# Weight sums of the block-product passes made in the pooling stage, and the passes' first operands split inside the mLSTM

## The chip, the cores and the metric

The kernel runs on one core of a Trainium2 chip. The metric is the device time of one execution in microseconds (us); the figure for a kernel is the median of its runs. A profiled execution of its own gives the trace from which all durations are read. The core's engines are TensorE (PE, matmuls and transposes, its weight loads shown as PEld), VectorE (DVE), ScalarE (ACT), GpSimd (POOL) and SyncE (SP). SP and ACT issue the DMAs, each in a queue of its own that runs in order.

## The reference

One layer of a decoder trunk over 4096 tokens of width 1024, in float32: a normalization, one input projection to 5120 columns, two branches that read it, one output projection, the residual, and a last normalization.

```python
u = rmsnorm(x, norm_w[l])
proj = u @ w_in[l]                      # 1024 -> 5 * 1024
pool_x, pool_z, m_x, m_z, m_o = ...     # 1024 columns each
y_pool = pool_mixer(pool_x, pool_w[l], pool_scale[l]) * jax.nn.silu(pool_z)
y_mlstm = mlstm_branch(m_x, m_z, m_o, ...)
mixed = jnp.concatenate([y_pool, y_mlstm], axis=-1)
x = x + mixed @ w_out[l]                # 2048 -> 1024
return rmsnorm(x, final_norm_w)

# in mlstm_branch, behind the chunkwise recurrence that gives h:
h = jax.nn.sigmoid(mo) * h
hn = ((h - mu) * lax.rsqrt(var + EPS)) * mh_norm_w     # mu, var per head
out = (hn + m_skip * xc) * jax.nn.silu(mz)
```

## The kernel before

**Precision.** A float32 product is made of three matmuls. `split` writes a tile as a rounded part `hi` (a cast on ACT, L110) and the remainder `lo` (a subtraction on DVE, L111); `mm3` (L117 to L119) adds hi·hi, hi·lo and lo·hi in PSUM.

**Stage A, pooling.** Eight blocks `b` of 512 tokens, each with eight column steps `j`. A block normalizes its tokens (`norm_u`), stores them as quarters into `us_d`, and makes the projections, the trailing window sums (DVE), the gate (ACT) and the product `sg`, which is stored into `yp_d`. Beside it `sums` (loads L493, subtractions L500 to L506 on POOL, stores L497) makes the sums of quarters that the block products need on the left side, for pairs of blocks that are done. The last of these jobs, `sums(yp_d[-1], 2)`, stands behind the loop.

**Stage B, mLSTM.** 32 chunks of 128 tokens. The weights `wm` of m_x are loaded through tiles `ws` (load L127, 16 loads of 256 KB, two buffers) and split. `project` loads `u` (L700), splits it (ACT L702, POOL L703) and multiplies; `front` and `back` are the two halves of a chunk, and the tuple `ORDER` says in which order the steps of front, back and projection are written down. L740 and L750 are the first map matmuls of `front`, L867 and L871 matmuls of `back`, L885 the activation that closes a head. In the last chunks, the generator `next_weights` takes the projection's place: it loads the first four right operands of C's first pass, as sums of up to four quarters, added on POOL (L129).

**Stage C, four passes.** `drive` runs the passes o1 (left side `yp_d`, with the first half of w_out), mo and mz (left side `us_d`, columns of w_in) and o2 (left side `ym_d`, second half of w_out). Each is a product of 2 x 2 blocks with seven block products (Strassen–Winograd, so that sums of quarters are needed on both sides), over four row bands `r`, seven products `i` and two halves `kh`: 14 half-steps a band, 24 matmuls of 512 columns each. For half-step `t` the left operand `sr` of half-step `t + 3` is loaded (`issue`, a DMA on ACT's queue, L223), and that of `t + 2` is split (`make`). `defer` puts work off to the end of the half-step. The right operands of the next pass are loaded in the last band of the pass before. `Pass.stage` (loads L155, POOL L159 to L162, stores L165) computes the sums of quarters of the right sides of mo and mz in bands 0 to 2 of o1, and those of o2 in mz, and stores them in `sums_...`; o1's own sums are made as they are loaded (L127, L129).

In pass mo an item `Head` finishes a block: tanh, product with `h`, the mean and variance (DVE L1035 to L1040 with a power on POOL L1038), and the normalization (ACT L1043). Each head block is then turned with transposes on TensorE (L1069), multiplied and added on DVE (L1071) with `xc` (L1062) and stored. The table `FREE_BANKS` says after which half-step of a band how many such turned tiles (four transposes each) are put into the program.

Two properties of the build matter for the order of the DMAs. A scheduler places instructions within each engine, so the order in a queue can differ from the order in the code. And the DMAs of SP and ACT share a small set of completion semaphores: the issue of a DMA waits for the landing of the one that used its semaphore last.

Of the kernel before, what the change touches and what calls it, by code (L numbers as in the profile page):

```python
# [17 lines left out]
P = 128  # L18
# [25 lines left out]
B_OF = (((1, 0, 0),),  # L44
        ((1, 1, 1), (-1, 0, 1), (1, 0, 0)),
        ((1, 1, 0),),
        ((1, 1, 1), (-1, 0, 1)),
        ((1, 0, 1), (-1, 0, 0)),
        ((1, 1, 0), (-1, 1, 1), (1, 0, 1), (-1, 0, 0)),
        ((1, 1, 1),))  # L50
SUM_OF = (None, 1, None, 2, 0, 3, None)

FREE_BANKS = {6: 2, 7: 2, 11: 3, 12: 3, 13: 3, 0: 3, 1: 2}
# [7 lines left out]
def tile_hybrid(  # L61
# [59 lines left out]
    def load_right(hi, lo, k, terms, sources, tile):  # L121

        acc = None
        for sign, kh, ch in terms:
            t = tile()
            rows, c0 = sources[ch]
            nc.sync.dma_start(out=t, in_=rows(k + 4 * kh)[:, c0:c0 + T])  # L127
            if acc is not None:
                nc.gpsimd.tensor_tensor(out=acc, in0=acc, in1=t, op=ALU.add if sign > 0 else ALU.subtract)  # L129
            else:  # L130
                acc = t
        split(acc, hi[:, k], lo[:, k])

    class Pass:


        def __init__(self, name, left, sources, items, by_row):

            self.name, self.left, self.sources, self.items, self.by_row = name, left, sources, items, by_row
            self.slots = {}  # L140
            self.sums = None
# [4 lines left out]
        def stage(self, k, tile):  # L146

            if self.sums is None:
                self.sums = dram.tile([4, P, 4, T], F32, name=f"sums_{self.name}")
            q = {}  # L150
            for kh in range(2):
                for ch in range(2):
                    rows, c0 = self.sources[ch]
                    q[kh, ch] = tile()
                    nc.sync.dma_start(out=q[kh, ch], in_=rows(k + 4 * kh)[:, c0:c0 + T])  # L155
            t3 = tile()
            yield
            b11, b12, b21, b22 = q[0, 0], q[0, 1], q[1, 0], q[1, 1]
            nc.gpsimd.tensor_tensor(out=t3, in0=b22, in1=b12, op=ALU.subtract)  # L159
            nc.gpsimd.tensor_tensor(out=b12, in0=b12, in1=b11, op=ALU.subtract)  # L160
            nc.gpsimd.tensor_tensor(out=b22, in0=b22, in1=b12, op=ALU.subtract)
            nc.gpsimd.tensor_tensor(out=b21, in0=b21, in1=b22, op=ALU.subtract)  # L162
            yield
            for i, t in enumerate((b12, b22, t3, b21)):
                nc.sync.dma_start(out=self.sums[i][:, k, :], in_=t)  # L165

        def load(self, i, pool, tag, tile):

            self.slots[i] = hi, lo = [pool.tile([P, 4, T], F32R, name=tag) for _ in range(2)]
            for k in range(4):  # L170
                if SUM_OF[i] is None or self.sums is None:
                    load_right(hi, lo, k, B_OF[i], self.sources, tile)
                elif k % 2 == 0:
                    raw = lo[:, k:k + 2].bitcast(F32)
                    nc.sync.dma_start(out=raw, in_=self.sums[SUM_OF[i]][:, k:k + 2, :])
                    split(raw, hi[:, k:k + 2], lo[:, k:k + 2])
                yield
# [34 lines left out]
    def drive(passes, ring, slot_pool, tile, psp, background):  # L212
# [13 lines left out]
        def make(t):  # L226
            if t < len(steps):
                hi, lo = got[t]
                split(lo.bitcast(F32), hi, lo)

        def load(p, i):
            for _ in p.load(i, *slot_pool(i), tile):
                pass
# [5 lines left out]
        def prefetch():  # L239
            while later and len(fetched) < 3:  # L240
# [4 lines left out]
        for t in range(AHEAD - 1):  # L245
            issue(t)
        for t in range(AHEAD - 2):
            make(t)
        for t, (n, r, i, kh) in enumerate(steps):
            p = passes[n]  # L250
            issue(t + AHEAD - 1)
            if n + r == 0:
                miss = [v for v in range(NP) if v not in p.slots]
                if miss and miss[0] <= t // 2 + 4:
# [11 lines left out]
            for q in range(4):  # L266
                ps = banks[chain, q]
                pairs = []
                for k in range(2):
                    kk = 2 * kh + k  # L270
                    if p.by_row:
                        pairs.append((tuple(z[:, k, q * P:(q + 1) * P] for z in s), tuple(z[:, kk, :] for z in w)))
                    else:
                        pairs.append((tuple(z[:, kk, q * P:(q + 1) * P] for z in w), tuple(z[:, k, :] for z in s)))
# [76 lines left out]
    ab = ExitStack()  # L351
    stp = ab.enter_context(tc.tile_pool(name="stp", bufs=4))
    wsp = ab.enter_context(tc.tile_pool(name="wsp", bufs=2))
# [29 lines left out]
    with tc.tile_pool(name="a_u", bufs=19) as up, \  # L383
# [124 lines left out]

        wz, wg = [], []
# [8 lines left out]
        job = None  # L518
        jobs = []
        for b in range(NB):  # L520
# [6 lines left out]
            for j in range(NJ):  # L527
# [8 lines left out]
                nc.gpsimd.tensor_copy(out=halo[:, j, :], in_=z[:, T:])  # L536
                pz = accp.tile([P, T], F32, name="acc")
# [36 lines left out]
        for _ in sums(yp_d[-1], 2):  # L574
# [3 lines left out]
    p_out1 = Pass("o1", yp_d, halves(out_rows(0), 0), [], True)  # L578
    with tc.tile_pool(name="b_one", bufs=1) as one, \
# [635 lines left out]
```

## Time and profile before

| | us |
|---|---|
| median of 3 runs (lowest, highest) | 3157.94 (3155.6, 3158.84) |
| profiled execution | 3153.02 |
| its span | 3151.3 |
| TensorE busy | 2919.7 |
| A's last matmul starts | 752.29 |
| first front of B | 820.85 |
| B's last matmuls start | 1757.23 |
| first matmul of C | 1770.93 |
| first matmul of mo, of mz, of o2 | 2115.1, 2495.7, 2815.9 |

The busy time of an engine is an average over stages that have different limits: in A TensorE is busy without a break, in B the small operations of the recurrence share the time, and in C TensorE is busy but for single stretches. In a row of the timeline the first two numbers are the start and the length, and the bracket at the end holds the idle time before and what ended it. In the rows of groups the last column is that idle time summed up.

### The profile page before, as it was taken

Reading aid. Unit: us, or ns where it says so; the run is one execution under the profiler, and the core shown is the slowest. Engines: PE = TensorE matmul, PEld = TensorE weight load, DVE = VectorE, ACT = ScalarE, POOL = GpSimd, SP = SyncE. Lnnn points to the kernel's source line nnn. Section 1 sums busy time; section 2 is a strip of 40 time slices with the busy share of each in tenths; the row PEclk is TensorE's granted clock in tenths of the full one; section 3 lists DMA queues with packets and bytes.
Section 4 is the critical chain, followed back from the end, with each engine's and each line's share of the span. In section 5 each row is a group of like instructions: output and inputs, shape, how many; then the busy total and the mean of one; then the engine's idle time right before and its main releaser. Section 6 shows DMA issues by size and latency. Waiting matters only on the chain. (4 is left out here: it accounts for less than half of the span.)

```text
span 3151.3 us, 45085 instructions
## 1 busy us (share of the span) xinstructions
PE 2919.7 (93%) x15912; PEld 2522.1 (80%) x15912; DVE 2089.8 (66%) x4160; ACT 1373.6 (44%) x2727; POOL 960.7 (30%) x1015
## 2 busy tenths in 40 slices
PE   7999999996989999999997788999998899998998
PEld 6888888885989989989897566887777688876887
DVE  6555555544578878888888553566667766575666
ACT  4222122211577677767666311235556633342332
POOL 1122333333245455445445432001111145321000
PEclk9999999998899999999998899999999999998999
DMA  6344455556121121111113688765666788786654
GB/s 211 124 153 159 155 181 184 184 174 201 46 64 51 48 68 48 61 55 51 61 58 111 227 309 268 238 225 192 209 218 230 260 273 302 260 290 208 213 208 157
DMA packets 256419, 530.55 MB, mean 168 GB/s; under 512 B 28352, under 2 KB 71872, under 8 KB 256192
## 3 DMA queue, kind: packets, MB, share of 16 engines
q1 hardware_dynamic: 223936, 410.21, 37.6%
q10 hardware_dynamic: 32256, 117.45, 11.9%
q8 instruction: 125, 2.05, 0.3%
q14 instruction: 102, 0.84, 0.1%
HBM read 334.63 MB, written 192.94 MB: 167 GB/s over the span
## 5 line engine op out<-in xcount | busy, mean ns | idle before, releaser
L117 PE MATMUL acc<-u,w 128*128 128x512 f32 (+1 forms) x2016 | 691.6, 343 | 2.2 <-ACT u L110 1.8
L119 PE MATMUL acc<-u,w 128*128 128x512 f32 (+1 forms) x2016 | 682.4, 339 | 0.0
L118 PE MATMUL acc<-u,w 128*128 128x512 f32 (+1 forms) x2016 | 680.7, 338 | 0.0
L117 PE MATMUL ps<-w,sr 128*128 128x512 f32 x1344 | 536.7, 399 | 44.4 <-ACT sr L110 29.6
L119 PE MATMUL ps<-w,sr 128*128 128x512 f32 x1344 | 533.6, 397 | 9.2 <-DVE sr L111 9.0
L118 PE MATMUL ps<-w,sr 128*128 128x512 f32 x1344 | 532.5, 396 | 0.0
L111 DVE TENSOR_TENSOR sr<-sr 128x1024 fp32r<-128x1024 f32 x224 | 293.5, 1314 | 304.3 <-ACT sr L110 299.4
L110 ACT CAST sr<-sr 128x1024 fp32r<-128x1024 f32 x224 | 234.2, 1048 | 552.0 <-PE ps L118 293.6
L117 PEld LDWEIGHTS acc<-u,w 128*128 128x128 f32 x2016 | 383.7, 190 | 44.3 <-ACT u L110 2.5
L118 PEld LDWEIGHTS acc<-u,w 128*128 128x128 f32 x2016 | 383.7, 190 | 40.3
L119 PEld LDWEIGHTS acc<-u,w 128*128 128x128 f32 x2016 | 383.5, 190 | 40.2
L117 PEld LDWEIGHTS ps<-w,sr 128*128 128x128 f32 x1344 | 257.9, 192 | 99.6 <-ACT sr L110 32.3
L119 PEld LDWEIGHTS ps<-w,sr 128*128 128x128 f32 x1344 | 257.1, 191 | 69.5 <-DVE sr L111 16.7
L118 PEld LDWEIGHTS ps<-w,sr 128*128 128x128 f32 x1344 | 257.6, 192 | 53.5 <-issue 0.5
L656 DVE SCALAR_TENSOR_TENSOR xc<-mx,col,xc 128x256 f32<-128x256 f32 x384 | 221.2, 632 | 55.4 <-POOL mx L715 46.4
L644 POOL TENSOR_TENSOR cs<-c,cs 128x516 fp32r<-128x516 f32 x124 | 176.4, 1422 | 204.2 <-ACT cs L643 181.7
L1038 POOL TENSOR_TENSOR rs<-rs,nhalf 128x2 f32<-128x2 f32 x64 | 56.0, 876 | 521.0 <-DVE mv L1035 325.9
L117 PE MATMUL ps<-sr,w 128*128 128x512 f32 x448 | 176.5, 394 | 4.3 <-ACT sr L110 3.3
L118 PE MATMUL ps<-sr,w 128*128 128x512 f32 x448 | 176.0, 393 | 1.4 <-DVE sr L111 1.4
L119 PE MATMUL ps<-sr,w 128*128 128x512 f32 x448 | 175.7, 392 | 0.0
L867 PE MATMUL mm<-va,st 128*128 128x258 f32 x384 | 85.6, 318 | 64.2 <-DVE st L111 42.6
L322 DVE TENSOR_TENSOR ch<-ps,ch 128x512 f32<-128x512 f32 x192 | 127.2, 681 | 14.4 <-PE ps L119 13.6
(211 smaller groups left out, 5192.8 us busy)
## 6 DMA issues: line engine op xcount, KB each, us to landing
sr<-us_d ACTq DMA_DIRECT2D x112, 512.0 KB, 5.0
us_d<-st SPq DMA_DIRECT2D x64, 512.0 KB, 2.7
sr<-yp_d ACTq DMA_DIRECT2D x56, 512.0 KB, 5.3
sr<-ym_d ACTq DMA_DIRECT2D x56, 512.0 KB, 4.5
st<-in_x_t_dram SPq DMA_DIRECT2D x32, 512.0 KB, 6.1
yp_d<-sg SPq DMA_DIRECT2D x64, 256.0 KB, 2.5
st<-us_d SPq DMA_DIRECT2D x32, 512.0 KB, 5.8
st<-yp_d SPq DMA_DIRECT2D x32, 512.0 KB, 5.8
```

The source lines that it names most:

```text
L110: nc.scalar.copy(out=hi, in_=raw)
L111: (eng or nc.vector).tensor_tensor(out=lo, in0=raw, in1=hi.bitcast(F32), op=ALU.subtract)
L117: nc.tensor.matmul(ps, lhsT=a[0], rhs=b[0], start=start and k == 0, stop=False, skip_group_check=skip)
L118: nc.tensor.matmul(ps, lhsT=a[0], rhs=b[1], start=False, stop=False, skip_group_check=skip)
L119: nc.tensor.matmul(ps, lhsT=a[1], rhs=b[0], start=False, stop=stop and k == n - 1, skip_group_check=skip)
L322: nc.vector.tensor_tensor(out=v(t), in0=ps, in1=v(t), op=ALU.add)
L644: nc.gpsimd.tensor_tensor(out=t[:, 1], in0=cst[h], in1=t[:, 0].bitcast(F32), op=ALU.subtract)
L656: nc.vector.scalar_tensor_tensor(out=a[:, t], in0=m[:, t, i:i + TB], scalar=conv_w[:, jj * 4 + i:jj * 4 + i + 1], in1=a[:, t], op0=ALU.mul ...
L867: nc.tensor.matmul(nps, lhsT=wt[:, w, h, :], rhs=vh[v], start=i == 0, stop=first and i == 2)
L1038: nc.gpsimd.tensor_tensor(out=rs, in0=rs, in1=nhalf[:, 0:2], op=ALU.pow)
```

## The change

The sums of quarters of all four right sides are made in A: a generator `right_sums` is advanced 14 times in each block from the second on, with the two buffers `ws`. `Pass.stage` goes, and `Pass.load` reads the stored sums. A's last job of left sums is made in C (`last_sums`, band 1 of o1, two parts of four loads of 256 KB). `next_weights` becomes `next_operands`, which also loads and splits the left operands of C's first three half-steps inside B. `drive` hands out the splits of right operands at the end of the half-step. `FREE_BANKS` turns the heads in other half-steps. The pools `st` and `ws`, shared by A and B before, are made for each stage, and one pool `xu` of twelve tiles serves B's `u` and C's `x`.

```diff
-FREE_BANKS = {6: 2, 7: 2, 11: 3, 12: 3, 13: 3, 0: 3, 1: 2}
+FREE_BANKS = {7: 4, 12: 4, 13: 3, 0: 1, 1: 4}
...
         def load(self, i, pool, tag, tile):
             self.slots[i] = hi, lo = [pool.tile([P, 4, T], F32R, name=tag) for _ in range(2)]
+            if SUM_OF[i] is not None:
+                for k in (0, 2):
+                    nc.sync.dma_start(out=lo[:, k:k + 2].bitcast(F32), in_=self.sums[SUM_OF[i]][:, k:k + 2, :])
+                return [lambda k=k: split(lo[:, k:k + 2].bitcast(F32), hi[:, k:k + 2], lo[:, k:k + 2])
+                        for k in (0, 2)]
...
         def prefetch():
-            while later and len(fetched) < 3:
+            while later and len(fetched) < 4:
...
-        for t in range(AHEAD - 1):
-            issue(t)
-        for t in range(AHEAD - 2):
-            make(t)
+        for t, pairs in enumerate(first):
+            got[t] = tuple([pair[v] for pair in pairs] for v in range(2))
...
+        def right_sums():
+            t, v = (wsp.tile([P, T], F32, name="ws") for _ in range(2))
+            for p in (p_out1, p_o, p_z, p_out2):
+                for k in range(4):
+                    def get(dst, kh, ch):
+                        rows, c0 = p.sources[ch]
+                        nc.sync.dma_start(out=dst, in_=rows(k + 4 * kh)[:, c0:c0 + T])
+                    def less(n, a, b):
+                        nc.gpsimd.tensor_tensor(out=a, in0=a, in1=b, op=ALU.subtract)
+                        nc.sync.dma_start(out=p.sums[n][:, k, :], in_=a)
+                    get(t, 0, 1)
+                    get(v, 0, 0)
+                    yield
+                    less(0, t, v)
+                    get(v, 1, 1)
+                    yield
...
+                if b and (j + 1) % 4:
+                    next(weights, None)
...
+                if b:
+                    next(weights, None)
...
-        for _ in sums(yp_d[-1], 2):
+        for _ in weights:
             pass
...
+    xu = ctx.enter_context(tc.tile_pool(name="xu", bufs=12))
+            tc.tile_pool(name="b_st", bufs=4) as stp, \
+            tc.tile_pool(name="b_ws", bufs=2) as wsp, \
...
-        def next_weights():
-            for i in range(4):
-                yield from p_out1.load(i, w1p, "w1", u_tile)
+        def next_operands():
+            for i in range(4):
+                todo = p_out1.load(i, w1p, "w1", x_tile)
+                yield
+                for n, f in enumerate(todo):
+                    f()
+                    if n == 1 and len(todo) > 2:
+                        yield
+            for t in range(AHEAD - 1):
+                pairs = []
+                for k in range(2):
+                    hi, lo = x_tile(F32R), x_tile(F32R)
+                    nc.sync.dma_start(out=lo.bitcast(F32), in_=yp_d[0][t // 2][:, 2 * (t % 2) + k, :])
+                    pairs.append((hi, lo))
+                first.append(pairs)
+            yield
+            for pairs in first:
+                for hi, lo in pairs:
+                    split(lo.bitcast(F32), hi, lo)
+                yield
...
-        todo = {0: [p.stage(k, x_tile) for p in (p_o, p_z) for k in range(4)],
-                2: [p_out2.stage(k, x_tile) for k in range(4)]}
+        def last_sums():
+            for k in (2, 3):
+                q = {}
+                for name in ("a11", "a12", "a21", "a22"):
+                    q[name] = x_tile()
+                    nc.sync.dma_start(out=q[name], in_=yp_d[-1][A_OF.index(name)][:, k, :])
+                yield
+                put_sums(yp_d[-1], k, q["a11"], q["a12"], q["a21"], q["a22"], x_tile, nc.gpsimd, store)
+                yield
...
+            if (n, r) == (0, 1) and m in (2, 4, 8, 10):
+                next(more)
```

The change moves instructions at three places of which the prediction speaks. At the turn from A to B, SP's queue of before holds this (`yp_d` is the result of A, `st` the tiles of the left sums, `ws` B's weights before their split, `u` its inputs, `st<-in_qkv_cols` the maps of q, k and v):

```order
L127 DMA ws<-in_w_in_dram 128x512 x4
L560 DMA yp_d_79<-sg 128x512
...
L127 DMA ws<-in_w_in_dram 128x512 x2
L612 DMA bif<-in_b_if_dram 128x8
L620 DMA ws<-in_w_if_dram 128x24x8
L623 DMA bvg<-in_qkv_cols_dram 128x8x128
...
L700 DMA u<-us_d_72 128x2x256
...
L493 DMA st<-yp_d_79 128x1024 x3
L497 DMA yp_d_79<-st 128x1024 x2
...
L623 DMA st<-in_qkv_cols_dram 128x1024 x3
L700 DMA u<-us_d_72 128x2x256 x4
```

The changed kernel has there (`xu` are B's inputs now):

```order
L470 DMA yp_d_79<-st 128x1024 x2
L605 DMA ws<-in_w_in_dram 128x512 x2
L565 DMA yp_d_79<-sg 128x512
L626 DMA bif<-in_b_if_dram 128x8
L637 DMA st<-in_qkv_cols_dram 128x1024
...
L637 DMA st<-in_qkv_cols_dram 128x1024 x2
...
L637 DMA bvg<-in_qkv_cols_dram 128x8x128
L730 DMA xu<-us_d_72 128x2x256
```

The left sums (L493, L497) have gone from the place ahead of B's inputs, and the 16 weight loads, which were spread over A's last block, now all come at the turn, mixed with the inputs; the tiles `ws` of B lie in memory over weights of A, so that the first of these loads waits for A's last matmul.

At the turn from B to C, ACT's stream of before is (`mx<-mm,r` is the last head, `sr` the left operands):

```order
L885 ACTIVATE mx<-mm,r 128x256 x3
L223 DMA sr<-yp_d_76 128x1024 x3
L110 CAST sr<-sr 128x1024 x2
L223 DMA sr<-yp_d_76 128x1024
L110 CAST w_18941<-x 128x512 x4
L110 CAST sr<-sr 128x1024
```

and that of the changed kernel:

```order
L915 ACTIVATE mx<-mm,r 128x256 x3
L189 DMA sr<-yp_d_76 128x1024 x2
L104 CAST w_19116<-w_19117 128x1024 x2
L104 CAST sr<-sr 128x1024
L189 DMA sr<-yp_d_76 128x1024
```

The loads and splits for the first three half-steps no longer stand between the last head and C's first matmul; the first `sr` that is loaded there belongs to the fourth half-step.

In pass mo, TensorE's stream around the start of a band is, before (`ps<-ident,ch` are transposes of heads, `ps<-w,sr` the matmuls):

```order
L119 MATMUL ps<-w_20823,sr 128x512
L1069 MATMUL ps<-ident,ch 128x128 x3
L117 MATMUL ps<-w_20823,sr 128x512
...
L1069 MATMUL ps<-ident,ch 128x128 x2
...
L1069 MATMUL ps<-ident,ch 128x128
L118 MATMUL ps<-w_20824,sr 128x512
```

and in the changed kernel:

```order
L113 MATMUL ps<-w_21259,sr 128x512
L1094 MATMUL ps<-ident,ch 128x128 x12
L111 MATMUL ps<-w_20828,sr 128x512
...
L1094 MATMUL ps<-ident,ch 128x128 x4
...
L1094 MATMUL ps<-ident,ch 128x128 x16
L111 MATMUL ps<-w_20908,sr 128x512
```

The transposes came in twos and threes among the matmuls of the band's first two half-steps; now they stand in groups between half-steps, 12 at the band's end, 4 behind its first half-step and 16 behind its second.

More of the change, by code (lines that the diff above doesn't have):

```diff
@@ L119, in mm3 @@
             nc.tensor.matmul(ps, lhsT=a[1], rhs=b[0], start=False, stop=stop and k == n - 1, skip_group_check=skip)
[L121 to L132, printed above, removed]
     class Pass:
@@ L140, in __init__ @@
             self.slots = {}
-            self.sums = None
+            self.sums = dram.tile([4, P, 4, T], F32, name=f"sums_{name}")
         def ready(self, r, i):
             pass
[L146 to L165, printed above, removed]
@@ L180, in tile_hybrid @@
+            kh, ch = B_OF[i]
+            rows, c0 = self.sources[ch]
+            raws = []
+            for k in range(4):
+                raws.append(tile())
+                nc.sync.dma_start(out=raws[k], in_=rows(k + 4 * kh)[:, c0:c0 + T])
+            return [lambda k=k: split(raws[k], hi[:, k], lo[:, k]) for k in range(4)]
     deferred = []
@@ L226, in make @@
         def make(t):
-            if t < len(steps):
+            if len(first) <= t < len(steps):
                 hi, lo = got[t]
@@ L231, in load, with splits @@
         def load(p, i):
-            for _ in p.load(i, *slot_pool(i), tile):
-                pass
+            def splits(todo):
+                for f in todo:
+                    f()
+            todo = p.load(i, *slot_pool(i), tile)
+            defer(lambda: splits(todo))
         later, fetched = [], []
@@ L518, in tile_hybrid @@
         job = None
+        weights = right_sums()
         jobs = []
@@ L591, in tile_hybrid @@
             for k in range(4):
-                load_right(*wm[i], k, ((1, i % 2, i // 2),), halves(in_rows, 2 * D), ws_tile)
+                raw = ws_tile()
+                r0, c0 = (k + 4 * (i % 2)) * P, 2 * D + i // 2 * T
+                nc.sync.dma_start(out=raw, in_=w_in[r0:r0 + P, c0:c0 + T])
+                split(raw, wm[i][0][:, k], wm[i][1][:, k])
         def proj_part(ps, j, u, part):
@@ L1075, in turned @@
                 return fetch, finish
+            return [turned(jj) for jj in range(4)]
         class Mixed(Item):
@@ L1136, in slot_pool @@
             return (w1p, "w1") if i < 4 else (w2p, "w2")
-        fw = one.tile([P, D], F32, name="fw")
         p_out1.items = [Sum(q, x) for q in range(4)]
-        p_o = HeadPass("mo", us_d, halves(in_rows, 4 * D), [Head(q) for q in range(4)], True)
-        p_z = Pass("mz", us_d, halves(in_rows, 3 * D), [Mixed(c) for c in range(4)], False)
-        p_out2 = Pass("o2", ym_d, halves(out_rows(D), 0), [Final(q, r_d) for q in range(4)], True)
-        todo = {0: [p.stage(k, x_tile) for p in (p_o, p_z) for k in range(4)],
-                2: [p_out2.stage(k, x_tile) for k in range(4)]}
-        def background(n, r, m):
-            if n in todo and r < NR - 1 and todo[n]:
-                if m in (2, 7, 11) if n == 0 else m in (1, 7):
-                    next(todo[n][0])
-                elif m in (4, 9, 13) if n == 0 else m in (3, 9):
-                    next(todo[n][0])
-                    job = todo[n].pop(0)
-                    defer(lambda: next(job, None))
-            if (n, r, m) == (2, 0, 0):
-                nc.sync.dma_start(out=fw, in_=final_w.partition_broadcast(P))
-        drive([p_out1, p_o, p_z, p_out2], ring, slot_pool, x_tile, psp, background)
+        p_o.items = [Head(q) for q in range(4)]
+        p_o.ready = heads_ready
+        p_z.items = [Mixed(c) for c in range(4)]
+        p_out2.items = [Final(q, r_d) for q in range(4)]
+        fw = []
+        def last_sums():
[4 more added lines that the diff above has]
+                    nc.sync.dma_start(out=q[name], in_=yp_d[-1][A_OF.index(name)][:, k, :])
+                yield
+                put_sums(yp_d[-1], k, q["a11"], q["a12"], q["a21"], q["a22"], x_tile, nc.gpsimd, store)
+                yield
+        more = last_sums()
+        def background(n, r, m):
+            if (n, r) == (0, 1) and m in (2, 4, 8, 10):
+                next(more)
+            if (n, r, m) == (3, 0, 2):
+                for h in range(2):
+                    fw.append(x_tile())
+                    nc.sync.dma_start(out=fw[h], in_=final_w[:, h * T:(h + 1) * T].partition_broadcast(P))
+        drive([p_out1, p_o, p_z, p_out2], ring, slot_pool, x_tile, psp, background, first)
 def kernel(**inputs):
```

92 lines of the change are left out of this document (43 added, 49 removed).

## The prediction

> **What bounds the kernel now.** I read the page from the top, then windows of the span stage by stage, then the waits inside the stages that lose time.
>
> ```profile
> PE 2919.7 (93%) x15912; PEld 2522.1 (80%) x15912; DVE 2089.8 (66%) x4160; ACT 1373.6 (44%) x2727; POOL 960.7 (30%) x1015
> PE   7999999996989999999997788999998899998998
> PEclk9999999998899999999998899999999999998999
> ```
>
> TensorE is the bound: 93% busy, and where its row falls below 9 the granted clock falls too. So only time in which TensorE waits, or runs at a reduced clock, can be won. The windows tell where that is. The first three lines below are the pooling stage A (to 752.7 us), the gap behind it, and the end of the mLSTM B; the others are bands of the passes C, cut at each band's first matmul.
>
> ```profile
> 700.00:750.00 50.00, 50.00 (x222) 41.42 (x221) 24.82 (x35) 12.46 (x22) 14.62 (x15) 1.00 0.54 183
> 750.00:800.00 50.00, 24.37 (x113) 22.39 (x111) 10.48 (x21) 8.08 (x32) 14.32 (x17) 0.60 0.61 199
> 1700.00:1750.00 50.00, 32.62 (x210) 30.13 (x210) 42.93 (x116) 30.87 (x78) 24.16 (x24) 0.83 0.20 65
> 1771.00:1854.00 83.00, 80.34 (x337) 64.94 (x338) 52.54 (x59) 21.29 (x26) 40.13 (x26) 0.96 0.91 319
> 1854.00:1963.00 109.00, 86.66 (x337) 66.67 (x337) 42.28 (x52) 15.73 (x15) 31.08 (x20) 0.91 0.85 283
> 1963.00:2039.00 76.00, 76.00 (x337) 62.92 (x336) 41.09 (x53) 14.81 (x15) 0.00 (x0) 1.00 0.75 247
> 2115.00:2200.00 85.00, 82.66 (x387) 67.61 (x385) 61.05 (x135) 47.11 (x70) 10.60 (x12) 1.00 0.60 200
> 2200.00:2294.00 94.00, 86.62 (x400) 69.71 (x399) 66.31 (x162) 52.62 (x82) 13.04 (x16) 0.98 0.64 212
> 2294.00:2391.00 97.00, 90.27 (x406) 72.72 (x405) 66.48 (x162) 53.05 (x83) 13.47 (x16) 0.95 0.64 208
> 2391.00:2496.00 105.00, 91.35 (x401) 73.12 (x400) 79.75 (x178) 64.71 (x101) 14.96 (x16) 0.93 0.76 251
> 2496.00:2579.00 83.00, 80.00 (x354) 64.99 (x354) 58.40 (x89) 38.07 (x55) 22.00 (x15) 0.99 0.82 266
> 2816.00:2911.50 95.50, 80.25 (x338) 64.61 (x337) 62.07 (x81) 27.67 (x43) 24.40 (x18) 0.91 0.65 211
> ```
>
> (Columns: window, its length, busy time of PE, PEld, DVE, ACT, POOL, then granted clock, DMA share, GB/s.) A band is 336 matmuls in 14 half-steps; undisturbed it takes 76 us (third band of pass o1), which is 0.2266 us a matmul and 5.4 us a half-step. Over that floor pass o1 loses 7 us in band 0 and 33 in band 1; pass mo 9, 18, 21 and 29; the first band of mz 7; the first of o2 19.5. A itself loses nothing (50.00 of 50.00).
>
> **Step 1, end of B to C.**
>
> ```profile
> 1757.23 0.90 PE L871 MATMUL mm<-cs,qi 128*128 128x258 f32 x6
> 1770.93 0.79 PE L117 MATMUL ps<-w,sr 128*128 128x512 f32 x1 [12.80 <-ACT sr L110]
> 1776.63 0.63 PE L117 MATMUL ps<-w,sr 128*128 128x512 f32 x1
> 1777.05 0.52 PE L118 MATMUL ps<-w,sr 128*128 128x512 f32 x1
> 1778.33 0.39 PE L117 MATMUL ps<-w,sr 128*128 128x512 f32 x1
> 1778.55 0.39 PE L118 MATMUL ps<-w,sr 128*128 128x512 f32 x1
> 1758.81 0.47 ACT L885 ACTIVATE mx<-mm,r 128x256 f32<-128x256 f32 x1 [0.64 <-DVE r L879]
> 1761.63 2.43 ACTq L223 DMA_DIRECT2D sr<-yp_d  x3
> 1769.84 1.04 ACT L110 CAST sr<-sr 128x1024 fp32r<-128x1024 f32 x1 [10.55 <-DMA sr<-yp_d]
> ```
>
> C's first matmul waits for a load of `sr` that is issued only at 1761.63, and its split. Afterwards the first three left operands are loaded and split inside B, and the first matmul needs only the last head's activation (1758.81 + 0.47), which frees PSUM: start near 1759.4, **−11.5**. After the long wait matmuls follow each other at 0.42 us until 1777 and at 0.22 from there; some 15 slow ones cost 15 × 0.21 = 3.2. With about 1.3 us of idle in place of 12.8 I count that slow start as gone too. In band 0 another 2.7 us of idle (83.00 − 80.34) goes with its 14 loads for four-term sums and three staging jobs. The fourth left operand is still loaded at C's start, but has three half-steps (16 us) against some 8 that the row shows from issue to cast. B itself trades POOL additions for six splits on ACT, at 30.87 of 50 busy: nothing, ±2. Sum **−17** (−19 to −13).
>
> On that slow start the Trainium skill, "TensorE: Matmul & The Clock Gate", Part 1 (The HAM clock gate), says that an idle window of about 3.4 us halves the clock and a busy one restores it. The spacing 0.42 against 0.22 behind a 12.80 us wait agrees. By it the short idle time that is left keeps the clock up and the term stays as above; if any idle time lowered the clock, it would be −14.
>
> **Step 2, band 1 of o1.**
>
> ```profile
> DVE sr L111 <- ACT sr L110: 72.0, 12, 16.7
> ACT sr L110 <- DMA x<-in_w_in_dram: 29.0, 2, 16.8
> ACT sr L110 <- DMA sums_mz<-x: 19.1, 2, 13.5
> 1887.63 6.12 SPq L165 DMA_DIRECT2D sums_mz<-x  x4
> ```
>
> ScalarE, which issues the `sr` loads, is held by the staging transfers: a load's issue waits for earlier transfers of SP's queue that share its completion semaphore, and SP itself stands behind POOL's subtractions. Staging leaves C altogether; in its place come two jobs (`last_sums`: 8 loads of 256 KB, 8 to 10 POOL operations, stores). Band 2 of before, with two staging jobs, ran at the floor: its 76.00 us are what band 1 becomes if two jobs are harmless. I take **−28** of the 33 (−33 to −15, the low end half of the loss kept).
>
> **Step 3, heads in mo and the first band of mz.**
>
> ```profile
> L1069 PE MATMUL ps<-ident,ch 128*128 128x128 f32 x240 | 44.4, 297 | 29.4 <-ACT ch L1043 16.2 <-ACT sr L110 4.2 <-DVE mv L1035 2.9
> 2216.50 0.38 PE L1069 MATMUL ps<-ident,ch 128*128 128x128 f32 x2
> ```
>
> Transposes of the heads stand in TensorE's order before matmuls that could run, and wait there for the normalized head. Band 0 of mo, which has some 50 transposes (387 − 337) and none of an earlier band, loses 9 us, 2.3 of them idle: 0.18 us a transpose. All 256 would cost 46 of the 84 us that these five bands lose (9 + 18 + 21 + 29 + 7); 38 are waits and the low clocks (0.98 to 0.93) behind them. Each group of 16 now comes half a step to two half-steps later: 16 after step 7, 16 after 12, 12 after 13, 4 and 16 after steps 0 and 1 of the next band. In band 1 the last of these transposes waited until 2216.5 for its head, 16.5 us after the band's start, and it will be asked for after two half-steps, at 10.9: up to 5.6 us a band can stay, some 2.5 if the heads come sooner with less in their way. I take **−28** (−38 to −12): 38 less 4 × 2.5; the low end keeps 5.6 in each band and a slow clock of 1 behind it.
>
> **Step 4, end of A to B.**
>
> ```profile
> 752.29 0.39 PE L119 MATMUL acc<-u,w 128*128 128x512 f32 x1
> 767.12 0.58 PE L117 MATMUL mm<-u,w 128*128 128x256 f32 x1 [14.43 <-ACT u L702]
> 820.85 2.02 PE L740 MATMUL map<-bvg,mx 128*128 128x136 f32 x16
> 765.87 1.27 SPq L493 DMA_DIRECT2D st<-yp_d  x3
> 708.82 1.32 ACT L110 CAST w<-ws 128x512 fp32r<-128x512 f32 x2 [5.70 <-DMA ws<-in_w_in_dram]
> 712.78 0.62 ACT L110 CAST w<-ws 128x512 fp32r<-128x512 f32 x1 [2.16 <-DMA ws<-in_w_in_dram]
> 716.70 0.62 ACT L110 CAST w<-ws 128x512 fp32r<-128x512 f32 x1 [2.25 <-DMA ws<-in_w_in_dram]
> ```
>
> From A's last matmul to the first front of B: 68.2 us. A's last sums stand in SP's queue ahead of B's inputs; they go. But B's 16 weight loads, which ran beside A's last block, now wait for A's last matmul, because their two buffers lie over A's weights. With two buffers they go in 8 rounds; a round took 3.9 us there (708.82, 712.78, 716.70), 6.3 at the most (5.70 + 0.62). At the 5.4 of the row on landing times in step 5, eight take 43, the gate weights in the same buffers half a round to a whole one (4), and 90 to 192 of the projection's matmuls (256 columns, half of 0.2266) remain behind them, 10 to 22: 43 + 4 + 16 = 63, **−5**. With the ends, 31 + 4 + 10 and 50 + 4 + 22, −23 to +8. The cover that is lost is A's last block; that is why this term may be a loss.
>
> **Step 5, inside A.**
>
> ```profile
> L465 POOL TENSOR_TENSOR w<-w 128x512 f32<-128x512 f32 x1 | 1.3, 1285 | 5.4 <-DMA w<-in_pool_scale_dram 5.4
> x<-in_w_in_dram SPq DMA_DIRECT2D x56, 256.0 KB, 5.4
> ```
>
> Added: 80 loads and 64 stores of 256 KB, and 64 subtractions at about 1.3 us (83 us of POOL). Over six blocks of 87 us that is 38 MB, or some 72 GB/s on top of 183 (the last window). Each subtraction comes about 6 us after its load is issued. DVE is at 25 of 50, POOL at 15. TensorE's cover is whole as long as a block's inputs arrive: **0** (0 to +5).
>
> **Step 6, the turn to o2.**
>
> ```profile
> PE ps L117 <- DVE ch L989: 14.5, 1, 14.5
> ```
>
> Its weight loads still stand in SP's queue behind the stores of the last mixed blocks, so the wait of 14.5 stays: 0 (±4). That `load` hands its splits out half a step later changes nothing that I can price: ACT already had them in that place.
>
> **Sum.** −17 − 28 − 28 − 5 = −78. The profiled execution took 3153.0 (span 3151.3), 4.9 under the median 3157.9 of the runs: 3157.9 − 78 ≈ **3080**.
>
> **The rivals.**
> *(a) Slower: A pays.* Mechanism: SP runs in order, and a store of a sum blocks it until POOL has subtracted. If each of a block's 14 rounds blocks SP for a load and a subtraction (5.4 + 1.3 us), SP is taken for 94 us of the block's 87, the next block's inputs come late, and TensorE waits at each boundary. It turns to a loss from 78 / 6 = 13 us a block; at 15 it gives 3080 + 90 = 3170. For it: SP stood 6.1 us before such stores in C (1887.63). Against: loads are issued a round ahead. 7%.
> *(b) The waits move, not go.* Band 1 keeps half its loss (+13), heads only win 12 (+16) since DVE (79.75 of 105) sets when they are ready, and B's weights cost +8 instead of −5: +42 if all, about 3108 if two of three. For it: ACT and DVE do the same work in C. 25%.
> *(c) All waits go*: −19 − 33 − 38 − 10 = −100, 3058. 15%.
> *(d) Bursts lower the clock.* If 16 transposes in a row let the granted clock drop as the wait at 1757 did, 16 bursts cost 3.2 each: 51, so 3131. Band 0 of mo had 48 transposes at a clock of 1.00, in groups of up to 12. 3%.
>
> On (d), the Trainium skill, "TensorE: Matmul & The Clock Gate", Part 4 (PE-mode transpose), says that transposes do not count as busy for the clock. By it a burst longer than its window would bring the 51 us of (d), and without it 0; no row of before has so long a burst, and the 1.00 of band 0 speaks against it.
>
> **How the numbers follow.** The forecast has 50% (own range 3066 to 3094); (b) 25, (c) 15, (a) 7, (d) 3. The range 3045 to 3125 leaves out (a), (d) and the far ends of the others. A measurement here can tell about 0.2% (6 us) from no change. Faster 0.90, the same 0.03 (between (a) and (b)), slower 0.07.
>
> **What would show it.** Step 1: the first `ps<-w` matmul within 2 us of B's last, at 0.22 us spacing from the start. Step 2: band 1 near 76 us, no ScalarE wait over 6 us in it. Step 3: idle before transposes under 10 us in all, and mo's bands near 88. Step 4: B's weight casts all behind A's last matmul, the first front some 63 us behind it. Step 5: PE 50.00 of 50.00 between 100 and 700 us. Step 6: a wait of about 14 us in o2's fifth half-step. PE idle at A's block boundaries would make the prediction wrong; so would transposes that still wait for normalized heads.

## The result, and the profile after

The changed kernel takes 3203.78 us (median of 4 runs, 3202.77 to 3206.32) against 3156.77 us of the kernel before, run beside it (3153.76 to 3158.84): a ratio of 1.0151, 95% interval 1.0133 to 1.0168. It is slower by 1.5%, where a gain of 2.5% was forecast. The profiled execution took 3204.38 us, its span is 3202.7, 51.4 more than before.

The first lines are windows of the changed kernel in stage A (same columns as in the prediction), then bands of C.

```profile
50.00:150.00 100.00, 100.00 (x445) 83.41 (x444) 57.33 (x92) 25.79 (x44) 16.89 (x22) 1.00 0.40 128
250.00:350.00 100.00, 81.06 (x343) 65.05 (x342) 46.10 (x60) 18.28 (x33) 38.34 (x33) 0.91 0.63 213
550.00:650.00 100.00, 82.68 (x339) 66.79 (x338) 44.33 (x59) 16.56 (x29) 39.80 (x34) 0.88 0.61 208
...
1861.60:1944.80 83.20, 78.56 (x336) 64.55 (x337) 46.33 (x56) 20.25 (x21) 11.24 (x8) 0.96 0.91 311
1944.80:2022.50 77.70, 76.50 (x337) 63.01 (x337) 39.85 (x50) 14.75 (x14) 0.00 (x0) 1.00 0.79 258
2174.80:2258.30 83.50, 81.80 (x381) 67.62 (x381) 60.11 (x134) 47.07 (x70) 10.61 (x12) 1.00 0.60 196
2258.30:2349.30 91.00, 86.69 (x404) 71.19 (x402) 65.91 (x163) 52.53 (x82) 13.62 (x16) 0.98 0.67 220
2442.30:2543.30 101.00, 90.50 (x402) 73.64 (x401) 76.35 (x176) 61.10 (x94) 15.12 (x16) 0.93 0.77 260
2543.30:2632.70 89.40, 82.94 (x360) 66.88 (x359) 59.96 (x94) 40.03 (x59) 10.52 (x8) 0.94 0.66 220
2865.00:2961.60 96.60, 79.93 (x337) 65.22 (x336) 63.21 (x81) 28.65 (x44) 27.18 (x19) 0.91 0.64 209
```

From the second block on, TensorE of stage A is busy 81 to 91 of 100 us where it was busy without a break, and the granted clock sinks to between 0.88 and 0.97. The first of these windows, in which 5 of the 64 sums are stored, is whole. Of C's bands, band 1 of o1 is 31 us shorter and those of mo are 1 to 4 us shorter; band 0 of o1 is as long as before, the first band of mz is 6 us longer and the first of o2 1 us. Now the timeline of TensorE at A's end, B's front and C's start, and its waits in A:

```profile
861.74 0.39 PE L113 MATMUL acc<-u,w 128*128 128x512 f32 x1
925.01 1.21 PE L770 MATMUL map<-bvg,mx 128*128 128x136 f32 x9
1861.62 0.50 PE L111 MATMUL ps<-w,xu 128*128 128x512 f32 x1 [1.21 <-ACT mx L915]
1861.95 0.40 PE L112 MATMUL ps<-w,xu 128*128 128x512 f32 x1
1862.19 0.39 PE L113 MATMUL ps<-w,xu 128*128 128x512 f32 x1
```

```profile
PE tp L393 <- ACT sq L104: 65.3, 6, 16.7
PE acc L112 <- DVE u L105: 19.1, 18, 6.0
```

TensorE's wait in A is for the most part, 65.3 of 85 us, six waits at the norm of the next block (L393, a sum over the squares of its tokens); another 19.1 us go to the splits of that block's `u`. Stage by stage, from such rows:

| from, to | before | after | difference | forecast |
|---|---|---|---|---|
| start, A's last matmul ends | 752.7 | 862.1 | +109.4 | 0 |
| A's last matmul, first front of B | 68.2 | 62.9 | −5.3 | −5 |
| first front, first matmul of C | 950.1 | 936.6 | −13.5 | −11.5 |
| pass o1 | 344.2 | 313.2 | −31.0 | −33.5 |
| pass mo and first band of mz | 463.7 | 457.8 | −5.9 | −28 |
| rest of mz, o2, to the last matmul | 561.3 | 558.6 | −2.7 | 0 |

B and C win 58 of the 78 us forecast; A loses 109.

### The profile page after: what moved, and what is told of

Read it like the earlier page. It is cut to its first block, busy times and chain, and to the rows that moved or that the text cites. A ratio compares the mean times of both kernels' runs of the same rounds, so it can differ in the third digit from the quotient of the medians.

```text
span 3202.7 us, 45056 instructions
## 1 busy us (share of the span) xinstructions
PE 2928.8 (91%) x15912; PEld 2531.3 (79%) x15912; DVE 2073.6 (65%) x4155; ACT 1376.8 (43%) x2722; POOL 939.0 (29%) x1007
## 5 line engine op out<-in xcount | busy, mean ns | idle before, releaser
L111 PE MATMUL ps<-w,sr 128*128 128x512 f32 x1320 | 520.6, 394 | 18.0 <-DVE ch L1016 13.6
L113 PE MATMUL ps<-w,sr 128*128 128x512 f32 x1320 | 517.6, 392 | 9.7 <-DVE sr L105 9.7
L112 PE MATMUL ps<-w,sr 128*128 128x512 f32 x1320 | 518.5, 393 | 0.0
L105 DVE TENSOR_TENSOR sr<-sr 128x1024 fp32r<-128x1024 f32 x221 | 285.9, 1296 | 266.6 <-ACT sr L104 265.7
L112 PE MATMUL acc<-u,w 128*128 128x512 f32 x1024 | 406.6, 397 | 19.1 <-DVE u L105 19.1
L111 PE MATMUL acc<-u,w 128*128 128x512 f32 x1024 | 404.4, 395 | 1.5 <-ACT u L104 1.5
L113 PE MATMUL acc<-u,w 128*128 128x512 f32 x1024 | 403.0, 394 | 0.0
L111 PEld LDWEIGHTS ps<-w,sr 128*128 128x128 f32 x1320 | 251.1, 190 | 72.2 <-DVE ch L1016 14.0
L113 PEld LDWEIGHTS ps<-w,sr 128*128 128x128 f32 x1320 | 250.4, 190 | 64.1 <-DVE sr L105 11.4
L111 PE MATMUL acc<-xu,w 128*128 128x256 f32 x992 | 294.8, 297 | 0.0
L112 PEld LDWEIGHTS ps<-w,sr 128*128 128x128 f32 x1320 | 250.8, 190 | 51.8
L113 PE MATMUL acc<-xu,w 128*128 128x256 f32 x992 | 287.2, 289 | 0.0
L112 PE MATMUL acc<-xu,w 128*128 128x256 f32 x992 | 284.5, 287 | 0.6 <-POOL xu L733 0.5
L112 PEld LDWEIGHTS acc<-u,w 128*128 128x128 f32 x1024 | 195.3, 191 | 70.1 <-DVE u L105 29.7
L111 PEld LDWEIGHTS acc<-u,w 128*128 128x128 f32 x1024 | 195.5, 191 | 43.4 <-ACT u L104 2.2
L670 DVE SCALAR_TENSOR_TENSOR xc<-mx,col,xc 128x256 f32<-128x256 f32 x384 | 220.9, 631 | 11.5 <-ACT xc L751 11.3
L113 PEld LDWEIGHTS acc<-u,w 128*128 128x128 f32 x1024 | 195.5, 191 | 39.8
L112 PEld LDWEIGHTS acc<-xu,w 128*128 128x128 f32 x992 | 193.8, 195 | 1.1 <-POOL xu L733 1.0
L111 PEld LDWEIGHTS acc<-xu,w 128*128 128x128 f32 x992 | 193.5, 195 | 1.2
```

The costliest lines, as they stand in the source:

```text
L105: (eng or nc.vector).tensor_tensor(out=lo, in0=raw, in1=hi.bitcast(F32), op=ALU.subtract)
L111: nc.tensor.matmul(ps, lhsT=a[0], rhs=b[0], start=start and k == 0, stop=False, skip_group_check=skip)
L112: nc.tensor.matmul(ps, lhsT=a[0], rhs=b[1], start=False, stop=False, skip_group_check=skip)
L113: nc.tensor.matmul(ps, lhsT=a[1], rhs=b[0], start=False, stop=stop and k == n - 1, skip_group_check=skip)
L670: nc.vector.scalar_tensor_tensor(out=a[:, t], in0=m[:, t, i:i + TB], scalar=conv_w[:, jj * 4 + i:jj * 4 + i + 1], in1=a[:, t], op0=ALU.mul ...
```

## The experiments

In all of them the kernel before, run beside them, took 3153 to 3158 us. A kernel that is given without a ratio ran once, and its stages are read from that run's trace. "Idle" is TensorE's waiting between 50 and 750 us, 85 us in the changed kernel and 0 before.

**Which part of a round costs A its time.** A round loads weights into one of two buffers, subtracts on POOL, and stores from SP. Three kernels take one thing out of it, two give it to another engine.

```diff
-                        nc.gpsimd.tensor_tensor(out=a, in0=a, in1=b, op=ALU.subtract)
                         nc.sync.dma_start(out=p.sums[n][:, k, :], in_=a)
```

> The 64 subtractions are left out (the stores write the loaded tiles, so the sums are not computed); all DMAs and SP's order stay. Theory SP: a store still waits for the load of its tile, so about 5 of 6.6 us a round stay; TensorE's idle time in A falls from 82 to some 40 to 60. Rival POOL: falls under 15. Rival traffic: stays near 82.

Measured 3125.3 us; A ends at 785.2, idle 27. The transfers alone, with SP's waits for them, cost A 32 us; the subtractions and the waits that they bring cost the other 77. The expectation of neither side was met exactly: more stays than POOL alone would leave, less than SP's order would.

```diff
-                        nc.sync.dma_start(out=p.sums[n][:, k, :], in_=a)
+                        nc.gpsimd.dma_start(out=p.sums[n][:, k, :], in_=a)
```

> The 64 stores of sums go out from POOL's own queue, so SP no longer stands before POOL's subtractions; rounds, bytes and POOL's work stay. Theory SP (SP's order, blocked by the stores, makes the token loads late): TensorE's idle time in A falls from 82 us to under 25. Rival POOL (halo copies stand behind subtractions that wait for their loads, and the block falls behind through them): idle time stays over 60. Rival traffic (the 38 MB themselves): stays near 82.

Measured 3219.0 us; idle 97, A ends at 878.8. It does not clear SP's order of blame by itself: with two buffers, SP then stood at the loads instead, until the last store from the buffer had landed (148 us) or POOL had done with it (55 us). It shows only that nothing is gained by taking the stores out of SP's queue.

```diff
-                        nc.gpsimd.tensor_tensor(out=a, in0=a, in1=b, op=ALU.subtract)
+                        nc.vector.tensor_tensor(out=a, in0=a, in1=b, op=ALU.subtract)
```

> The 64 subtractions of the sums run on DVE instead of POOL; loads, stores and their order in the code stay. Theory lockstep (a round holds SP until the subtraction of the tile before is done, and that waits for a load that SP could issue only then): a round still ties SP to load and subtraction, some 6 us, so TensorE's idle time in A stays at 40 to 80 of 82 us. Rival POOL alone (left sums and halo copies stand behind subtractions that wait): idle time falls to the 27 us of the kernel without subtractions, or under it.

Measured 3142.8 us; idle 25, A ends at 797.0, so that A loses 44 us instead of 109. The waits of SP's stores between 150 and 750 us, in this kernel and then in the changed one:

```profile
SPq L493 <- DVE ws L492: 138.0, 50, 9.5
```

```profile
SPq L493 <- POOL ws L492: 138.9, 29, 9.0
SPq L493 <- POOL halo L539: 62.9, 16, 9.2
SPq L493 <- POOL z L538: 13.5, 3, 4.7
```

SP stands before the stores for 147 us with DVE (9 us of it put down to other operations of DVE) and for 215 us with POOL (the last two rows are stores of sums too, put down to POOL's copies beside the subtractions). Two thirds of SP's waiting stay with DVE, and yet TensorE's idle time is down by 60 us. So most of the loss comes with the subtractions in POOL's order. This does not clear SP's order, which runs late as well when POOL does: in the changed kernel SP hardly ever waits for the products `sg` that it stores (8.9 us; 241.6 before, 73.6 with DVE), since they are done when it gets there. The changed kernel's waits of POOL between 150 and 750 us, and a stretch of its timeline, show how POOL comes to be late:

```profile
POOL ws L492 <- DMA ws<-in_w_in_dram: 143.4, 29, 12.9
POOL ws L492 <- DMA ws<-in_w_out_dram: 97.8, 20, 8.6
POOL halo L539 <- ACT z L537: 62.6, 7, 12.6
```

```profile
306.18 2.75 SPq L489 DMA_DIRECT2D ws<-in_w_in_dram  x2
311.26 1.48 POOL L492 TENSOR_TENSOR ws<-ws 128x512 f32<-128x512 f32 x1 [5.49 <-DMA ws<-in_w_in_dram]
312.77 0.33 SPq L493 DMA_DIRECT2D sums_mo<-ws  x1
313.19 2.56 SPq L489 DMA_DIRECT2D ws<-in_w_in_dram  x2
318.20 1.29 POOL L492 TENSOR_TENSOR ws<-ws 128x512 f32<-128x512 f32 x1 [4.72 <-DMA ws<-in_w_in_dram]
```

A round takes 6.9 us (311.26 to 318.20), of which POOL stands 4.7 before the load that SP issues only behind the store of the round before. (Over the whole of A there is a round every 10 us.) In 600 us POOL stands 241 us so, 49 times; with its work (some 38 of 100 us in the windows above, about 238) and its other waits it has no time left. What is behind it in its order comes late: the copies of the halo, on which DVE's window sums wait, the power in the norm (DVE waits 59.1 us for it, 6.8 before), and the left sums, whose four tiles the next block's tokens need. ScalarE is held as well: it can't fill its next tile `sg` until SP has stored an earlier one. Two waits of the changed kernel that have no counterpart before, and the wait that stood in the first one's place before:

```profile
DVE sum L551 <- POOL z L538: 120.0, 23, 12.2
ACT sg L545 <- DMA yp_d<-sg: 103.0, 15, 10.9
```

```profile
DVE sum L546 <- ACT z L534: 97.7, 36, 4.8
```

With the subtractions on DVE both waits are gone. That POOL's added work makes DVE's operations longer is not the cause: from 50 to 750 us DVE is busy 0.124 us for each matmul of A (326 us for 2616 matmuls), before 0.125 (387 for 3088). In the timeline, the token loads and the norm's matmul of one block:

```profile
293.44 1.89 SPq L378 DMA_DIRECT2D st<-in_x_t_dram  x3
308.24 1.52 PE L393 MATMUL tp<-sq,ones_r 128*128 128x512 f32 x2 [16.70 <-ACT sq L104]
```

TensorE came to this norm at 291.5 and the loads were issued at 293.4. Before the change the same loads stood at 260.6, ahead of a norm at 279.4.

The next kernel was meant to give POOL the work and not the waits:

```diff
-                        nc.gpsimd.tensor_tensor(out=a, in0=a, in1=b, op=ALU.subtract)
+                        for _ in range(2):
+                            nc.gpsimd.tensor_tensor(out=scr, in0=scr, in1=two, op=ALU.subtract)
```

> As the kernel without subtractions (the stores write the loaded tiles, the sums are not computed), but POOL does two subtractions of 256 columns on a tile of its own in place of each, so it has that work and never waits for a load. Theory wait (POOL's waits for loads, not its work, make A longer): TensorE's idle time in A stays near the 27 us of the kernel without subtractions (20 to 40). Rival work (83 us of POOL beside its own, or what its operations cost DVE): it goes up to 60 or more.

Measured 3180.5 us; between 150 and 750 us TensorE's idle time is 25, but this tells nothing of the question, as its windows show:

```profile
50.00:150.00 100.00, 83.86 (x350) 67.28 (x349) 55.46 (x71) 28.08 (x50) 77.14 (x95) 0.91 0.29 90
...
250.00:350.00 100.00, 89.75 (x387) 73.51 (x386) 46.42 (x65) 19.24 (x34) 25.08 (x25) 0.95 0.74 251
```

Work that waits for nothing was placed at the beginning of A (POOL 77 of 100 us), not beside the rounds. Inconclusive. The other way round works, since it keeps the waits that set the place:

```diff
-                        nc.gpsimd.tensor_tensor(out=a, in0=a, in1=b, op=ALU.subtract)
+                        nc.gpsimd.tensor_tensor(out=a[:, 0:8], in0=a[:, 0:8], in1=b[:, 0:8], op=ALU.subtract)
```

> The subtractions stay on POOL with their waits, but work on 8 of the 512 columns (the sums are not computed): POOL waits for every load, and so does SP for POOL, with hardly any work. Theory wait: TensorE's idle time in A stays near 82 us (70 or more). Rival work: it falls to the 27 us of the kernel without subtractions (under 40). In between, both count.

Measured 3167.9 us; idle 58, A ends at 829.8.

```profile
POOL ws L492 <- DMA ws<-in_w_in_dram: 145.9, 28, 11.5
POOL ws L492 <- DMA ws<-in_w_out_dram: 121.3, 24, 12.1
```

Both count. A's 109 us are in steps: transfers 32 (785.2), POOL's waits 45 (829.8), its work 32 (862.1). The last two are a rough split, since a subtraction of 8 columns still takes POOL 0.54 us, so that the 45 hold some work too.

**Does the pace of the rounds decide?** One kernel writes a block's rounds behind its token loads, one makes half the sums in A (o1 and mo) and the others in C.

```diff
-                if b and (j + 1) % 4:
+                if b and j >= 4:
                     next(weights, None)
```

> The rounds of a block (11) are all written behind the left sums and the token loads of that block, in its column steps 4 to 7, where the changed kernel spreads 14 over the block. Theory lockstep: 11 rounds of 6.6 us are 73 us in half a block of 44, so they run into the next block's first half and idle time stays over 50 us. Rival place (only rounds ahead of the token loads hurt): idle time falls under 20.

Measured 3206.7 us; A ends at 862.4, with the six waits in the same places. It doesn't tell the two theories apart, since the stores of sums start in the same stretches as in the changed kernel:

```text
stores per 50 us from 100 us on
changed kernel            5 3 8 2 7 3 7 4 5 6 4 6 4
written late              5 3 7 3 7 3 6 5 5 6 5 5 4
half of the sums, 6 a block   5 3 7 3 7 3 4
```

```diff
-            for p in (p_out1, p_o, p_z, p_out2):
+            for p in (p_out1, p_o):
...
-                if b:
+                if b and j < 6:
                     next(weights, None)
...
+            if n == 0 and r > 1 or n == 2 and r in (0, 1):
+                if m in (1, 7):
+                    next(todo[n][0])
```

> Only the sums of o1 and mo are made in A, at 6 rounds a block; those of mz are made in bands 2 and 3 of o1, those of o2 in bands 0 and 1 of mz (two jobs a band). Theory lockstep with a threshold (87 us of a block / 6.6 us = 13 rounds): 6 rounds take 40 us of SP's block and TensorE's idle time in A falls under 10; C stays within 10 of its 1330 us; the whole comes to 3095 to 3110, faster than before by 45 to 60. Rival (each round costs 1 us and more by itself, whatever their number): idle time in A stays at 35 to 45 for half the rounds, the whole at 3140 or more.

Measured 3158.8 us, ratio 1.0018 (1.0007 to 1.0028): no gain. A ends at 806.3, half of the loss for half of the sums, and all of its idle time lies before 420 us: six rounds a block in the code came out at the pace of before. Where the scheduler sets the order, the code's place for a round is no handle on its pace; the question of a threshold stays open. C pays 14 us for the sums that are made there again.

**The sums in B.** The rounds go from A to the mLSTM.

```diff
-                if b and (j + 1) % 4:
-                    next(weights, None)
...
-            for what in ORDER[n % 2]:
+            for at, what in enumerate(ORDER[n % 2]):
+                if n and at % 12 == 5:
+                    next(weights, None)
```

> The 80 rounds of loads, subtractions and stores of the weight sums run in the mLSTM (three rounds a chunk) instead of the pooling stage; all else is as in the changed kernel. Theory P (the pooling stage pays because SP, ACT's and POOL's orders there are full): stage A ends near 753 again, C keeps its 1330 us, and the whole comes to 3204 - 109 = 3095 plus what the mLSTM pays (0 to 25): 3095 to 3120. Rival (the loss in A is the moved buffers of A and B, not the sums): A still ends near 862 and the whole stays near 3200.

Measured 3160.6 us, ratio 1.0023 (1.0010 to 1.0036). A ends at 754.9, so the loss in A is the sums and not the moved buffers. But B, from its front to C, takes 1000.7 us instead of 936.6. POOL's waits in B:

```profile
POOL cs L650 <- ACT cs L649: 126.5, 49, 7.1
...
POOL st L335 <- DMA st<-in_w_out_dram: 62.8, 21, 8.1
POOL st L335 <- DMA st<-in_w_in_dram: 54.9, 22, 5.6
```

118 us of waits for loads, in the order in which the splits of the state (`cs`) stand. B pays 64 us, where 0 to 25 were expected. It is likely that the rounds do there what they did in A, but no run tests it.

**The heads.**

```diff
-FREE_BANKS = {7: 4, 12: 4, 13: 3, 0: 1, 1: 4}
+FREE_BANKS = {6: 2, 7: 2, 11: 3, 12: 3, 13: 3, 0: 3, 1: 2}
...
-            while later and len(fetched) < 4:
+            while later and len(fetched) < 3:
```

> The changed kernel with the table of before for the heads, and three instead of four fetched. If turning the heads later is worth what was forecast, pass mo and the first band of mz take 28 us longer than the 458 of the changed kernel. If it is worth the 6 us by which the traces differ, they take about 464, and if later turns even cost, less than 458.

Measured: mo and the first band of mz take 463.3 us against 457.8. Turning later is worth 5.5 us: 7.4 in mo, less 2 in the first band of mz. (The whole took 3218.8; of the other 9 us some 5 lie in A and 3 in o1.) The waits before the transposes of mo did not go; where they were 29.4 us in the row of step 3, they are 21.2 in the changed kernel:

```profile
L1094 PE MATMUL ps<-ident,ch 128*128 128x128 f32 x249 | 38.1, 293 | 21.2 <-ACT ch L1070 14.9 <-DVE ch L292 3.5 <-DVE xu L1096 2.4
```

```diff
-                for hh in range(2):
-                    nc.vector.bn_stats(out=stats[:, hh, :], in_=t[:, hh * DH:(hh + 1) * DH])
-                    nc.vector.bn_aggr(out=mv[:, hh, :], in_=stats[:, hh, :])
...
-                    nc.scalar.activation(out=hw, in_=hw, func=AF.Identity, scale=rs[:, hh:hh + 1], bias=nb[:, hh:hh + 1])
```

> The mean, variance and scaling of the heads are left out (the blocks are turned as they leave the gate), which shortens the way from a block's last matmul to its transposes; transposes, their evacuation and all transfers stay. If TensorE's remaining loss in mo is the wait for normalized heads and the slow clock behind it, idle time in mo falls from 24 to under 8 us, and mo with the first band of mz takes 458 - 30 = 428 or less. If it is the transposes themselves and their evacuation, it stays over 445.

Measured 416.8 us for these five bands, with 4.8 us of idle time. Bands 1 and 3 of mo and the first of mz:

```profile
2254.20:2337.60 83.40, 83.40 (x404) 69.89 (x402) 50.13 (x66) 35.49 (x50) 0.00 (x0) 1.00 0.73 239
...
2420.90:2509.60 88.70, 85.59 (x404) 70.95 (x402) 58.90 (x76) 46.19 (x64) 0.00 (x0) 0.98 0.84 283
2509.60:2590.10 80.50, 78.83 (x359) 65.30 (x358) 53.11 (x68) 33.47 (x46) 5.71 (x4) 1.00 0.75 245
```

Without the wait for a normalized head a band with 64 transposes (band 1) has no idle time at all and costs 7.2 us over the 76.2 of a band without (bands 2 and 3 of o1): 0.11 us a transpose, in bursts of 16, at a clock of 1.00. So 41 us (457.8 − 416.8) of waiting, and of the slow clock behind it, are still in the changed kernel. This kernel also has less work on DVE, 50 us in such a band instead of 66, so it does not tell how much of the 41 us is the length of the normalization itself and how much is DVE's load.

**C's fifth half-step.** ACT's timeline and TensorE's wait in the changed kernel:

```profile
1885.26 1.05 ACT L104 CAST w<-w 128x1024 fp32r<-128x1024 f32 x1 [7.45 <-DMA w<-sums_o]
1886.54 1.05 ACT L104 CAST w<-w 128x1024 fp32r<-128x1024 f32 x1 [0.23 <-DMA w<-sums_o]
1887.49 1.04 ACT L104 CAST sr<-sr 128x1024 fp32r<-128x1024 f32 x1
...
1888.75 0.79 PE L113 MATMUL ps<-w,sr 128*128 128x512 f32 x1 [4.63 <-DVE sr L105]
```

```diff
-                if miss:
+                if miss and miss[0] <= t // 2 + 4:
                     load(p, miss[0])
```

> The right operands 4 to 6 of o1 are loaded at C's half-steps 0, 2 and 4, as before the change, instead of 0, 1 and 2. Theory: the new wait in C's fifth half-step (12.4 us against 5.4) is a left operand's cast that stands on ACT behind the casts of right operand 5, whose load lands late; then the fifth half-step falls under 7 and band 0 of o1 under 78 us. Rival (the left operand itself comes late, behind the 12 loads of the residual): it stays at 12.

Measured: the wait falls from 4.63 to 1.81 us and band 0 from 83.2 to 78.4 us, a little over the 78 expected; the left operand did stand behind the casts. But band 1 goes from 77.7 to 81.8, and pass o1 gains 0.6 us. (The whole took 3210.6, since A ended 6 us later than in the changed kernel.)

**A version that beats both.** Subtractions on DVE with the loads at half-steps 0, 2 and 4, and then with half of the sums made in C as above.

```diff
-                        nc.gpsimd.tensor_tensor(out=a, in0=a, in1=b, op=ALU.subtract)
+                        nc.vector.tensor_tensor(out=a, in0=a, in1=b, op=ALU.subtract)
...
-                if miss:
+                if miss and miss[0] <= t // 2 + 4:
```

> Subtractions of the sums on DVE, and the right operands of o1 at half-steps 0, 2 and 4. The two parts add: A as with DVE (ends near 797), C some 7 us shorter: 3143 - 7 = 3136, faster than before by 0.4 to 0.7%.

Measured 3144.2 us, ratio 0.9961 (0.9948 to 0.9973). The two parts do not add: with DVE alone it took 3142.8. A ends at 800.7, 3.7 us later than there, and C is only 1.5 us shorter, where 7 were expected.

```diff
-            for p in (p_out1, p_o, p_z, p_out2):
+            for p in (p_out1, p_o):
```

> As the last, but only the sums of o1 and mo are made in A (on DVE), those of mz in o1, those of o2 in mz. A pays half of its 44 us: ends near 775; C pays the 14 us that it paid with these jobs on POOL: 3136 - 22 + 14 = 3128. If the loss of A goes with the rounds that are made there, A ends between 770 and 780; if the first rounds cost all of it, near 797.

Measured 3135.1 us (3129.4 to 3136.4) against 3157.7, ratio 0.9929 (0.9914 to 0.9944). Windows of its A, with sums and behind them, and of bands 0 and 1 of o1:

```profile
250.00:350.00 100.00, 95.25 (x409) 76.99 (x408) 54.99 (x75) 20.04 (x35) 31.31 (x28) 0.98 0.64 214
...
450.00:550.00 100.00, 100.00 (x442) 82.71 (x441) 52.35 (x68) 20.56 (x36) 30.95 (x27) 1.00 0.50 175
```

```profile
1776.50:1855.00 78.50, 76.62 (x337) 63.12 (x338) 43.41 (x52) 18.73 (x20) 17.67 (x12) 1.00 0.91 312
1855.00:1944.60 89.60, 81.30 (x337) 64.53 (x336) 42.45 (x54) 15.79 (x16) 11.14 (x8) 0.96 0.91 308
```

A ends at 783.3, a little later than the 770 to 780 expected. Band 1 of o1 loses 13 us again (89.6 against 76.2), and among its waits stands the one that step 2 of the prediction described:

```profile
ACT sr L104 <- DMA sums_mz<-xu: 28.3, 2, 14.4
```

## Why the prediction was wrong

- **Step 5, inside A, is the step that failed:** "Each subtraction comes about 6 us after its load is issued … TensorE's cover is whole as long as a block's inputs arrive: 0 (0 to +5)". Measured +109. The 6 us were taken from the spacing of the generator's steps in the code. With two buffers a load can go out only when the subtraction before it is done, and POOL reaches the next subtraction before that load has landed: it stood there 4.9 us a round on average. Counted as work, a round took 1.3 us of POOL (1.7 in the mean of the trace); counted with the wait it took 6.9, and POOL, busy 15 of 50 us before, had no room left. The step counted the added instructions on their engine, but not who stands behind them: the halo copies and the left sums, and through them the next block's tokens. It also counted 80 loads where the code makes 96, so that the transfers are 42 MB and not 38.
- **Rival (a)** named the sign, the round of 6.7 us (measured 6.9), the late inputs at the block boundaries and a loss of 15 us a block (measured 18), with 7%. It put the whole blame on SP's order. SP's order does carry part of the delay (the token loads stand in it behind the stores of the left sums), but with the subtractions on DVE SP still waits 147 us for them (215 with POOL), and A loses 44 instead of 109. "Against: loads are issued a round ahead" was the same misreading of the code's order.
- **Step 1** held in its main part: C's first matmul stands 1.21 us behind B's last work, and from the third on the spacing is 0.23 us. That the short idle time would leave the clock up came true. What was not seen is the new wait in the fifth half-step (4.63, with its slow clock about 7 us), so that band 0 of o1 won nothing, where some 5.5 us were forecast.
- **Step 2** was right: band 1 falls from 109 to 77.7 (−31.3; −28 forecast), and ScalarE's longest wait for a load in it is 6.6 us.
- **Step 3** failed too: −28 forecast, −5.9 measured. That the transposes wait for normalized heads was right; that turning them later takes these waits away was not (21.2 us stay in mo, under 10 were forecast). It took the place of the transposes for the lever. The waits go when the normalization is left out, which the change leaves alone, and the new places are only up to two half-steps later. A transpose costs 0.11 us and not 0.18, so that of the 84 us some 55 were waits and slow clocks, not 38; and 41 are still there.
- **Step 4** was right: front 62.9 us behind A's last matmul, forecast 63, with the 16 loads at the turn; the casts of the weights end 40 us behind that matmul (43 forecast), and the rest takes 23 (20).
- **Step 6** was right: the wait stays (13.6 us by the row of `ps<-w,sr` on the page, 14.5 before).
- **Rival (b)** came true in the heads, which won even less than the 12 us that it left them; band 1 and B's weights went as forecast.
- **Rival (d)**, that bursts of 16 lower the clock, is refuted by band 1 of mo in the kernel without normalization, which ran at 1.00.

What is settled: the loss is made by the rounds, about two thirds of it by the subtractions in POOL's order with their waits (77 us go without them, 65 with them on DVE), the rest by the transfers. Not settled: which path carries most of POOL's part to TensorE, the halo copies and the norm's power or SP's late stores and token loads; how the 32 us of the transfers divide between SP's order, the shared completion semaphores and the traffic itself; and whether a slower pace would cost less a round.

## What to carry to other kernels

A wait inside an engine's fixed order costs that engine like work: for every added instruction that reads a fresh load, count the load's landing time on its engine, and name what is queued behind it. How far a load is issued ahead is read from the built order or from buffers, not from the spacing in the code: with two buffers that are both in use, there is no ahead. And an engine that is idle much of the time, as POOL was here, is only a good place for such work if nothing on the critical path stands in its queue.

## What the runs showed of the hardware that was not expected

Transposes in bursts of 16 ran at 0.11 us each with the clock at 1.00. A slow stretch of A costs more than its idle time: 85 us of waits made A 109 us longer, with the granted clock at 0.88 to 0.97 in its windows.
